# A decoder trunk on one core: how the first head's wait is filled, and who turns the second norm's first token tile

## The chip, the core and the metric

The kernel runs on one core of a Trainium2 chip. The metric is the device time of one execution in microseconds (us). TensorE is called PE here, VectorE DVE, ScalarE ACT, GpSimd POOL and SyncE SP, as in the profile.

## What is computed

With a depth of one, the trunk is one attention layer, a SwiGLU feed-forward layer and a last norm, over 512 tokens of width 2048 in float32:

```python
hn = rmsnorm(x, mix_norm_g)
h = x + nsa_mixer(hn, rel_bias, ...)      # 16 heads, 4 groups
h = h + swiglu(rmsnorm(h, ffn_norm_g), ffn_w_in, ffn_w_out)
return rmsnorm(h, final_norm_g)
```

Each head of the mixer has three branches (compressed, selected, window). Their probabilities are weighted by gates and multiplied with the values; the heads' outputs go through `w_out`. The feed-forward part needs the normed `h` with its channels on the partitions, so every token tile of 128 x 2048 must be turned once after the second norm.

## The kernel before

Every float32 product is made of three matmuls of split operands: `three` (lines 342 to 346) multiplies high by high, high by low and low by high. A weight tile (a granule of 128 x 1024) is loaded, copied to its high part on ACT (L102) and to its low part on DVE (L103) by `Weights.split`. `Weights.ahead(n)` splits until n granules beyond the one in use are ready, and issues the loads of the next three on the queue `W.queue`; `take` calls it.

The mixer's second stage interleaves two things by hand. The dense stream (`dense`) is a generator of projections for later heads: it yields after each chunk (three matmuls of 512 columns, or six of 256), counts 650 ns for it, and has 32 chunks in each pair of query heads, keys or values. `pump(h, step)` draws chunks until their count reaches a goal that grows by 20800 ns for each head of 12 steps, so one head takes exactly 32 chunks. The attention of a head is a chain:

- `scores(h, t)`: PE writes the scores of token tile t into the PSUM tile `s`, which all tiles share; DVE adds the bias and finds the maximum (L907), and ACT takes the exponential (L909).
- `finish(h, t)`: DVE scales the probabilities and turns them in blocks of 32 x 32 (L922), and SP stores them to DRAM (`d_p`, L924).
- `fetch(t)`: a DMA brings them back with the blocks in place (`ptr`, L928).
- `turn(h, b, kt)`: ACT makes the high part (`pth`, L945), DVE the low part (`ptl`, L949).
- `values(h, b, kt)`: PE multiplies with the values into `o`.

For head 0 this chain has no head before it. The kernel calls its four `scores` in a row with `pump(-1, ...)` between them, which gives 3, 3, 2 and 2 chunks, then 4 before the first scores of head 1 and 5 after them. The loop over heads draws nothing more until step 4 of head 0. `W.queue` is POOL from before the first scores on, and POOL also issues the fetches of tiles 3 and 2 of head 0.

The second norm follows the output projection. For each token tile t, four PSUM banks take the last heads' products (48 matmuls), `add` puts them on the residual `acc`, ACT sums the squares, `rstd` makes the factor and `scaled` (L314) writes the normed tile to `xn`. The next tile's matmuls are interrupted twice by `turned`, which transposes eight blocks of 128 x 128 of the tile before on PE (L322); ACT and DVE split the result into `n2_hl` (L328, L333). Tile 3 is turned inside the first feed-forward projection, which reads tiles 0 and 1 first.

Of the kernel before, what the change touches and what calls it, by code (L numbers as in the profile page):

```python
# [10 lines left out]
F32 = mybir.dt.float32  # L11
# [32 lines left out]
TP_GAP, HN_GAP = 40, 48  # L44
RESYNC = 14
PT_STEP = 224
SPREAD, N_WARM = UL, 17


# [166 lines left out]
def nsa_block(ctx: ExitStack, tc: tile.TileContext, x, rel_bias, mix_g, ffn_g, fin_g, w_in, w_out,  # L216
# [25 lines left out]
    d_o = [dram.tile([4, 128, S], F32, name=f"d_o{i}") for i in range(3)]  # L242
    d_h = dram.tile([S, 256 * N_SPILL], F32, name="d_h")
    d_r = dram.tile([NT, 128, D], F32, name="d_r")
    d_a = dram.tile([NF // 2, 128, 5 * S], F32, name="d_a")
    d_w = {j: dram.tile([128, 4, 2, 256], F32, name=f"d_w{j}") for j in G1 + G2}

# [34 lines left out]
    def tok(t):  # L282
        return slice(128 * t, 128 * (t + 1))
# [22 lines left out]
    def rstd(ss):  # L306
        y = smallp.tile([128, 1], F32, name="rs")
        run(rstd_steps(ss, y))
        return y
# [427 lines left out]
    with ExitStack() as st2:  # L737
# [22 lines left out]
        def qpair(h0):  # L760
            ps = proj2()
            end = q_out(ps, h0)
            for i in range(4):
                last = ws(ps, i, W.take(), end=end)
                for n, c in enumerate(last):
                    yield c
                    if h0 == H - 2 and i and n in (2, 4, 6):
                        reload_o(3 * i + n // 2 - 4)
                    if h0 == H - 2 and i == 3 and n in (0, 3):
                        split_o(n // 3)  # L770
            done["n"] += 1
            yield None
# [78 lines left out]

        def pump(h, step):
            at = h + (step + 4) / STEPS
            goal = 20800 * min(at, 13) + 22500 * max(at - 13, 0)
            while done["ns"] < goal:
                c = next(stream, "end")
                if c == "end":
                    return
                done["ns"] += c or 0
# [112 lines left out]
                split_from(o, hn_h[:, h], hn_l[:, h])  # L972
            del HS[h]

        W.queue = pool
        load_bias(0)
        load_bias(1)
        for i in range(4):
            scores(0, 3 - i)
            if i > 1:  # L980
                fetch(5 - i, pool)
            if i:
                finish(0, 4 - i)
            pump(-1, min(9 + i, 11.7))
        finish(0, 0)
        fetch(1)
        fetch(0)
        pump(0, 1)
        scores(1, 3)
        for b in range(2):  # L990
            turn(0, b, 3)
        pump(0, 3)
        for h in range(H):
            seq = [(b, kt) for kt in (3, 2, 1, 0) for b in (0, 1)] + [(-1, 0)]
            for i in range(STEPS):
                if i == 4:
                    load_bias(h + 2)
                if i == 2 and h:
                    fetch(0)
                if i < 9 and (h or i > 1):  # L1000
                    turn(h, *seq[i])
                if i == 8 and h + 1 < H:
                    fetch(3)
                    fetch(2)
                if i == 11 and h + 1 < H:
                    fetch(1)
                if i == 0 and h:
                    finish(h, 0)
                if h + 1 < H:
                    if i == 2:  # L1010
                        drain_to(needed(h + 1))
                    if i % 3 == 2 and h + i > 2:
                        scores(h + 1, 3 - i // 3)
                    elif i % 3 == 0 and i:
                        finish(h + 1, 4 - i // 3)
                if 2 <= i < 10 or i == 11:
                    if i == 2 and h % HPG == 0:
                        drain_to(h)
                    values(h, *seq[min(i - 2, 8)])
                    if i == 11:  # L1020
                        head_out(h)
                pump(h, i)
        W.queue = nc.sync
        drain_to(100)
    mixer.close()
# [27 lines left out]
    with tc.tile_pool(name="n2", bufs=1) as n2:  # L1053
        act(warm, epsc, AF.Sqrt)
        gb2 = n2.tile([128, D], F32, name="gb2")
        nc.scalar.dma_start(gb2, ffn_g[0:1, :].to_broadcast([128, D]))
        xn = n2.tile([128, D + 64], F32, name="xn")
        wr_h = n2.tile([128, 6, 1024], F32R, name="wr_h")
        wr_l = n2.tile([128, 6, 1024], F32R, name="wr_l")
        for i in range(6):  # L1060
            W.place[marks[0] + i] = wr_h[:, i], wr_l[:, i]
        for cb in (2, 3):
            po = out_tiles()
            cs = [slice(256 * c, 256 * (c + 1)) for c in (2 * cb - 4, 2 * cb - 3)]
            parts = [n2.tile([128, 1024], F32, name="back", bufs=3).rearrange("p (t c) -> p t c", t=NT) for _ in cs]
            for i in range(6):
                if i == 2:
                    for c, p in zip(cs, parts):
                        nc.sync.dma_start(p, d_h[:, c].rearrange("(t p) c -> p t c", p=128))
                w = W.take(2 if cb == 2 else min(2 + i, 6))  # L1070
                for t in range(NT):
                    tokmajor(po[t], w, heads(i), i == 0, i == 5, t)
            W.ahead(3)
            for t in range(NT):
                add(t, cb, po[t])
            for c, p in zip(cs, parts):
                dve.tensor_tensor(acc[:, :, c], acc[:, :, c], p, op=OP.add)
        w8 = []
        for t in range(NT):
            ss = smallp.tile([128, 4], F32, name="ss4")  # L1080
            po = out_tiles()
            for cb in range(4):
                for i in range(2):
                    if t == 0:
                        w8.append(W.take(7 - len(w8)))
                    tokmajor(po[cb], w8[2 * cb + i], heads(6 + i), i == 0, i == 1, t)
                add(t, cb, po[cb])
                if t == NT - 1 and cb == 3:
                    W.ahead(3)
                if cb == 3:  # L1090
                    pool.dma_start(d_r[t], acc[:, t])
                if t and cb in (1, 2):
                    turned(xn, (2 * cb - 2, 2 * cb - 1), t - 1)
                junk = ps3.tile([128, 512], F32, name="pp")
                act(junk, acc[:, t, 512 * cb:512 * (cb + 1)], AF.Square, accum_out=ss[:, cb:cb + 1])
            next(ready_made)
            scaled(acc[:, t], rstd(ss), gb2, xn)
            W.ahead(min(t, 2))
        firstp.close()
        pf0 = ctx.enter_context(tc.tile_pool(name="pf0", bufs=2, space=PSUM))  # L1100
        pa = [ps3.tile([128, 512], F32, name="pp") for _ in range(2)]
        gs = []
        for i in range(4):
            gs.append(W.take(min(2, 3 - i)))
            run(ws(pa, i, gs[i], 0, 256, of=n2_hl))
            if i in (1, 2):
                turned(xn, (2 * i - 2, 2 * i - 1), 3)
        act(warm, epsc, AF.Silu)
# [628 lines left out]
```

## Time and profile before

| | |
|---|---|
| median of 3 runs | 2097.61 us (2096.29 to 2098.01) |
| the profiled execution | 2096.34 us |
| its span, first to last instruction | 2094.6 us |
| around the span | 1.74 us |
| PE busy | 2075.1 us (99%) |
| DVE busy | 1627.6 us (78%) |
| ACT, POOL busy | 948.6 us (45%), 278.2 us (13%) |
| DMA, mean | 204 GB/s |

Matmuls are pipelined: the record of one lasts longer than its share of the engine. In the timeline the distance between two starts is what counts, and a stall is the part of that distance beyond the usual one. A bracket at the end of a timeline row gives the idle time before it and what ended it.

### The profile page before, as it was taken

The page shows a single profiled execution, that of the slowest core. Times are in us where ns is not written, and L with a number is a line of the kernel's source. Part 1 is how long each engine was busy: PE and PEld are TensorE (multiplying, and loading weights), DVE is VectorE, ACT ScalarE, POOL GpSimd, SP SyncE. Part 2 cuts the span into 40 slices and gives each one's busy share as a digit, 9 for nine tenths or more (in the row PEclk, how much of TensorE's full clock was granted, in tenths as well). Part 3 has the DMA queues.
Part 4 walks back from the last instruction along what each step waited for, and adds up shares of the span by engine and source line. Part 5 has one row for each costly group of instructions (what it writes and reads, how often), then busy time and mean ns, then how long its engine had stood idle before and what let it go on. Part 6 is the DMA issues. An engine that isn't in the chain of part 4 may idle for free.

```text
span 2094.6 us, 39078 instructions
## 1 busy us (share of the span) xinstructions
PE 2075.1 (99%) x15236; PEld 1954.1 (93%) x15236; DVE 1627.6 (78%) x2705; ACT 948.6 (45%) x1524; POOL 278.2 (13%) x404
## 2 busy tenths in 40 slices
PE   9999999999999999999999999999999999999998
PEld 7898788898989889899999999999999999999997
DVE  5565777777786457898888888888888688697767
ACT  6344554555455234434434344344343455464445
POOL 2000111111111001022222132221211100000000
PEclk9999999999999999999999999999999999999999
DMA  7555767666677658578878778788755686685667
GB/s 238 171 157 155 198 192 201 189 193 191 204 218 208 240 179 213 151 209 231 216 205 224 205 223 220 196 232 215 199 158 157 208 267 187 194 295 151 196 204 279
DMA packets 321799, 427.68 MB, mean 204 GB/s; under 512 B 40300, under 2 KB 249900, under 8 KB 320973
## 3 DMA queue, kind: packets, MB, share of 16 engines
q1 hardware_dynamic: 261020, 292.18, 43.9%
q0 software_dynamic: 59696, 131.16, 25.8%
q8 instruction: 119, 1.95, 0.4%
q10 hardware_dynamic: 896, 1.84, 0.2%
q14 instruction: 68, 0.55, 0.1%
HBM read 363.12 MB, written 130.13 MB: 235 GB/s over the span
## 4 chain that ended last, share of the span: by engine, by line
PE 67%; DVE 1%; DMA 1%; ACT 0%; issue 0%; SPq 0%; DVEq 0%; ACTq 0%
PE f L344 18%; PE f L345 18%; PE f L346 18%; PE proj L344 2%; PE proj L346 2%; PE proj L345 2%; PE pp L344 1%; PE pp L346 1%; PE pp L345 1%; PE po L346 1%; PE po L344 1%; PE po L345 1%; DMA tlo<-d_w 1%; PE pp L322 0%; DMA tlo<-in_ffn_w_out 0%
## 5 line engine op out<-in xcount | busy, mean ns | idle before, releaser
L103 DVE TENSOR_TENSOR wlo<-raw,whi 128x1024 fp32r<-128x1024 f32 (+2 forms) x223 | 247.5, 1112 | 123.6 <-ACT whi L102 123.0
L102 ACT ACTIVATE whi<-raw 128x1024 fp32r<-128x1024 f32 (+2 forms) x223 | 215.9, 970 | 218.8 <-PE f L346 57.0
L346 PE MATMUL f<-hn_h,wlo 128*128 128x256 f32 x984 | 271.6, 276 | 0.0
L344 PE MATMUL f<-hn_h,whi 128*128 128x256 f32 x984 | 271.6, 276 | 0.0
L345 PE MATMUL f<-hn_l,whi 128*128 128x256 f32 x984 | 271.6, 276 | 0.0
L1229 ACT ACTIVATE whi<-raw 128x1024 fp32r<-128x1024 f32 x123 | 126.2, 1058 | 303.0 <-DVE raw L1125 299.6
L1125 DVE TENSOR_TENSOR tlo<-tt,thi 128x1536 fp32r<-128x1536 f32 (+1 forms) x83 | 145.4, 1752 | 77.8 <-ACT thi L1234 77.3
L344 PE MATMUL proj<-hn_h,whi 128*128 128x512 f32 x504 | 199.9, 397 | 0.0
L346 PE MATMUL proj<-hn_h,wlo 128*128 128x512 f32 x504 | 196.9, 391 | 0.0
L345 PE MATMUL proj<-hn_l,whi 128*128 128x512 f32 x504 | 196.9, 391 | 0.0
L345 PEld LDWEIGHTS f<-hn_l,whi 128*128 128x128 f32 x984 | 184.7, 188 | 0.0
L344 PEld LDWEIGHTS f<-hn_h,whi 128*128 128x128 f32 x984 | 184.7, 188 | 0.0
L346 PEld LDWEIGHTS f<-hn_h,wlo 128*128 128x128 f32 x984 | 184.7, 188 | 0.0
L1234 ACT ACTIVATE thi<-tt 128x1536 fp32r<-128x1536 f32 x82 | 121.9, 1486 | 72.9 <-PE f L345 61.3
L345 PE MATMUL f<-tlo,slot 128*128 128x256 f32 (+1 forms) x546 | 151.7, 278 | 0.0
L344 PE MATMUL f<-thi,slot 128*128 128x256 f32 (+1 forms) x546 | 151.6, 278 | 0.0
L346 PE MATMUL f<-thi,slot 128*128 128x256 f32 (+1 forms) x546 | 151.6, 278 | 0.0
L346 PE MATMUL proj<-whi,hn_l 128*128 128x256 f32 (+2 forms) x496 | 146.1, 295 | 2.9 <-DVE hn_l L810 2.9
L1125 DVE TENSOR_TENSOR wlo<-raw,whi 128x1024 fp32r<-128x1024 f32 x123 | 147.0, 1223 | 1.1 <-ACT whi L1229 1.1
L344 PE MATMUL proj<-whi,hn_h 128*128 128x256 f32 (+2 forms) x496 | 146.6, 295 | 0.8 <-ACT hn_h L809 0.8
L345 PE MATMUL proj<-wlo,hn_h 128*128 128x256 f32 (+2 forms) x496 | 145.6, 294 | 0.0
L345 PE MATMUL f<-wlo,slot 128*128 128x256 f32 (+1 forms) x432 | 121.4, 281 | 0.0
(406 smaller groups left out, 6459.9 us busy)
## 6 DMA issues: line engine op xcount, KB each, us to landing
raw<-in_ffn_w_in SPq DMA_DIRECT2D x135, 512.0 KB, 5.1
d_w<-in_ffn_w_out POOLq DMA_DIRECT2D x80, 512.0 KB, 8.4
rawx<-in_ffn_w_in SPq DMA_DIRECT2D x41, 512.0 KB, 4.8
raw<-in_ffn_w_out SPq DMA_DIRECT2D x73, 256.0 KB, 3.9
tlo<-d_w SPq DMA_DIRECT2D x73, 256.0 KB, 4.3
d_a<-d_a POOLq DMA_DIRECT2D x120, 128.0 KB, 5.7
slot<-d_a SPq DMA_DIRECT2D x18, 768.0 KB, 6.7
raw<-in_nsa_w_in POOLq DMA_DIRECT2D x24, 512.0 KB, 5.0
```

Source lines behind the costliest of these rows:

```text
L102: self.nc.scalar.activation(hi[:, :n], src, AF.Copy)
L103: self.nc.vector.tensor_tensor(lo[:, :n], src, hi[:, :n].bitcast(F32), op=OP.subtract)
L344: mm(o, ah, bh, start=start, stop=False, skip_group_check=True)
L345: mm(o, ah, bl, start=False, stop=False, skip_group_check=True)
L346: mm(o, al, bh, start=False, stop=stop, skip_group_check=True)
L1125: dve.tensor_tensor(o, a, b, op=OP.subtract)
L1229: act(h, r, AF.Copy)
L1234: act(h, ttf, AF.Copy)
```

## The change

Two edits. The first head's filling: the chunks between the four scores become 4, 2, 3 and 2, then 4, then 7 after the first scores of head 1, and `pump` draws again from step 2 of head 0 on. A lead of 3900 ns, which shrinks to nothing at head 13, is added to the goal of `pump`. The raw weights of this stretch are loaded on SP; POOL takes over after it. One granule's split is moved by hand from a `take` to a call of `W.ahead(2)` after the last scores of head 0.

The second norm's first tile: `first_turned` writes the normed tile in an order of channels such that DVE's transposition of 32 x 32 blocks (128 x 2048 in one instruction), four stores to DRAM and one load put the channels on the partitions. The load goes to `acc[:, 0]`, which is free after its own store to `d_r`. `first_hi` then makes both parts, two instructions on ACT and two on DVE, at the end of tile 2 and inside tile 3. The 16 transposes of this tile on PE and its splits go away. Two calls of `W.ahead` are shifted to make room.

```diff
+LEAD = 3900
+    d_n = dram.tile([4, 32, 4, 512], F32, name="d_n")
-                last = ws(ps, i, W.take(), end=end)
+                last = ws(ps, i, W.take(1 if h0 == 2 and i == 1 else 2), end=end)
         def pump(h, step):
             at = h + (step + 4) / STEPS
-            goal = 20800 * min(at, 13) + 22500 * max(at - 13, 0)
+            pump_to(20800 * min(at, 13) + 22500 * max(at - 13, 0) + LEAD * max(1 - at / 13, 0))
-        W.queue = pool
         load_bias(0)
         load_bias(1)
         for i in range(4):
             scores(0, 3 - i)
             if i > 1:
                 fetch(5 - i, pool)
             if i:
                 finish(0, 4 - i)
-            pump(-1, min(9 + i, 11.7))
+            if i == 3:
+                W.ahead(2)
+            pump_to(650 * (4, 6, 9, 11)[i])
         finish(0, 0)
         fetch(1)
         fetch(0)
-        pump(0, 1)
+        pump_to(650 * 15)
         scores(1, 3)
         for b in range(2):
             turn(0, b, 3)
-        pump(0, 3)
+        pump_to(650 * 22)
+        W.queue = pool
...
-                pump(h, i)
+                if h or i > 1:
+                    pump(h, i)
...
+        def first_turned(y):
+            v = xn[:, :D].rearrange("p (m k j) -> p k m j", m=4, j=32)
+            a, g = (x.rearrange("p (k m j) -> p k m j", m=4, j=32) for x in (acc[:, 0], gb2))
+            for m in range(4):
+                dve.scalar_tensor_tensor(v[:, :, m], a[:, :, m], y, g[:, :, m], op0=OP.mult, op1=OP.mult)
+            b = back[:, :2].rearrange("p b c -> p (b c)")
+            dve.transpose(b, xn[:, :D])
+            for a in range(4):
+                nc.sync.dma_start(d_n[:, :, a].rearrange("m j f -> j m f"),
+                                  b[32 * a:32 * a + 32].rearrange("j (m f) -> j m f", m=4))
+            nc.sync.dma_start(acc[:, 0], d_n.rearrange("m j a f -> (m j) (a f)"))
+        def first_hi():
+            v = acc[:, 0].rearrange("p (a k s) -> p k a s", a=4, s=32)
+            h, l = (x[:, :, tok(0)].rearrange("p k (a s) -> p k a s", a=4) for x in n2_hl)
+            k2 = (slice(0, 8), slice(8, 16))
+            for k in k2:
+                act(h[:, k], v[:, k], AF.Copy)
+            for k in k2:
+                dve.tensor_tensor(l[:, k], v[:, k], h[:, k].bitcast(F32), op=OP.subtract)
+                yield
...
-                if t and cb in (1, 2):
+                if t > 1 and cb in (1, 2):
                     turned(xn, (2 * cb - 2, 2 * cb - 1), t - 1)
...
+                if t == NT - 1 and cb == 2:
+                    next(parts_of_first)
+                    W.ahead(2)
             next(ready_made)
-            scaled(acc[:, t], rstd(ss), gb2, xn)
-            W.ahead(min(t, 2))
+            if t:
+                scaled(acc[:, t], rstd(ss), gb2, xn)
+            else:
+                first_turned(rstd(ss))
+            if t == 2:
+                parts_of_first = first_hi()
+                next(parts_of_first)
+            W.ahead(min(t, 1))
```

## Rows read from the trace of the kernel before

**Rows 1.** The page, busy time of each engine with its share of the span.
```profile
PE 2075.1 (99%) x15236; PEld 1954.1 (93%) x15236; DVE 1627.6 (78%) x2705; ACT 948.6 (45%) x1524; POOL 278.2 (13%) x404
```

**Rows 2.** Waits of PE in the whole run: total us, times, longest us.
```profile
PE proj L346 <- DVE hn_l L810: 2.9, 2, 2.2
PE o L344 <- ACT pth L945: 1.7, 1, 1.7
```

**Rows 3.** Windows: stretch, length, busy us by engine, PEclk, DMA share, GB/s.
```profile
350.00:400.00 50.00, 50.00 (x245) 42.19 (x244) 39.12 (x108) 25.06 (x68) 5.99 (x8) 1.00 0.66 189
...
608.00:611.50 3.50, 3.50 (x17) 3.50 (x18) 2.16 (x8) 2.42 (x8) 0.00 (x0) 0.52 0.93 286
```

**Rows 4.** Timeline of PE, first head: start, duration, line, output<-inputs, idle before.
```profile
203.15 0.39 PE L346 MATMUL proj<-hn_h,wlo 128*128 128x512 f32 x1
204.41 0.40 PE L344 MATMUL s<-k0h,qh 128*128 128x288 f32 x1 [0.88 <-DVE mx L907]
...
209.57 0.40 PE L346 MATMUL proj<-hn_h,wlo 128*128 128x512 f32 x1
210.73 0.40 PE L344 MATMUL s<-k0h,qh 128*128 128x288 f32 x1 [0.77 <-DVE mx L907]
...
216.77 0.39 PE L344 MATMUL proj<-hn_h,whi 128*128 128x512 f32 x1
...
219.97 0.39 PE L346 MATMUL proj<-hn_h,wlo 128*128 128x512 f32 x1
220.98 0.30 PE L344 MATMUL o<-pth,v0h 128*128 128x128 f32 x1 [0.62 <-issue]
...
221.76 0.28 PE L346 MATMUL o<-pth,v0l 128*128 128x128 f32 x1
223.70 0.38 PE L344 MATMUL o<-pth,v0h 128*128 128x256 f32 x1 [1.66 <-ACT pth L945]
224.16 0.39 PE L345 MATMUL o<-ptl,v0h 128*128 128x256 f32 x1
```

**Rows 5.** Timeline of DVE, first head.
```profile
210.59 0.08 DVE L907 DVE_READ_ACCUMULATOR2_ANT mx<- 128x1 f32 x1
...
220.91 0.49 DVE L949 TENSOR_TENSOR ptl<-ptr,pth 128x128 fp32r<-128x128 f32 x2 [1.22 <-ACT pth L945]
```

**Rows 6.** Timeline of ACT (first row) and POOL, first head.
```profile
223.23 0.72 ACT L945 ACTIVATE pth<-ptr 128x256 fp32r<-128x256 f32 x2 [1.20 <-DMA ptr<-d_p]
...
217.56 0.76 POOL L928 DMA_DIRECT2D ptr<-d_p  x1 [2.35 <-DMA d_p<-p]
218.31 1.52 POOL L86 DMA_DIRECT2D raw<-in_nsa_w_in  x2
```

**Rows 7.** Timeline of PE, second norm, tile 1 and the first feed-forward projection.
```profile
773.46 0.39 PE L346 MATMUL proj<-wr_h,hn_l 128*128 128x512 f32 x1
773.69 1.03 PE L322 MATMUL pp<-ident,xn 128*128 128x128 f32 x8
774.48 0.48 PE L344 MATMUL po<-wr_h,hn_h 128*128 128x512 f32 x1
...
812.36 0.81 PE L322 MATMUL pp<-ident,xn 128*128 128x128 f32 x6
```

**Rows 8.** DVE: transposition durations min/median/max ns; then the second norm's timeline.
```profile
L922 DVE STREAM_TRANSPOSE p<-p x64: 578/980/1381, 208.5 to 676.5; 128x1152 f32<-128x1152 f32 x16, 128x896 f32<-128x896 f32 x16, 128x640 f32<-128x640 f32 x16, 128x384 f32<-128x384 f32 x16
...
771.38 2.74 DVE L314 SCALAR_TENSOR_TENSOR xn<-acc,rs,gb 128x512 f32<-128x512 f32 x4
...
806.90 0.69 DVE L1039 TENSOR_TENSOR acc<-acc,po 128x512 f32<-128x512 f32 x1 [1.13 <-PE po L346]
...
810.09 2.74 DVE L314 SCALAR_TENSOR_TENSOR xn<-acc,rs,gb 128x512 f32<-128x512 f32 x4
```

**Rows 9.** DMA issues: output<-input, queue, count, KB each, us to landing (203 to 230, 765 to 800).
```profile
d_p<-p SPq DMA_DIRECT2D x4, 48.0 KB, 5.5
...
d_r<-acc POOLq DMA_DIRECT2D x3, 1024.0 KB, 5.2
```

More of the change, by code (lines that the diff above doesn't have):

```diff
@@ L853, in pump, with pump_to @@
             at = h + (step + 4) / STEPS
-            goal = 20800 * min(at, 13) + 22500 * max(at - 13, 0)
+            pump_to(20800 * min(at, 13) + 22500 * max(at - 13, 0) + LEAD * max(1 - at / 13, 0))
+        def pump_to(goal):
             while done["ns"] < goal:
@@ L1057, in nsa_block @@
         xn = n2.tile([128, D + 64], F32, name="xn")
+        back = n2.tile([128, 3, 1024], F32, name="back")
+        n_back = iter((0, 1, 2, 0))
+        def first_turned(y):
[18 more added lines that the diff above has]
+                yield
         wr_h = n2.tile([128, 6, 1024], F32R, name="wr_h")
@@ L1064, in nsa_block @@
             cs = [slice(256 * c, 256 * (c + 1)) for c in (2 * cb - 4, 2 * cb - 3)]
-            parts = [n2.tile([128, 1024], F32, name="back", bufs=3).rearrange("p (t c) -> p t c", t=NT) for _ in cs]
+            parts = [back[:, next(n_back)].rearrange("p (t c) -> p t c", t=NT) for _ in cs]
             for i in range(6):
```

## The prediction

> **What bounds the kernel.** I read the page first: PE is busy for 2075.1 of 2094.6 us [rows 1], so 19.5 us of idle time is all that a better order can give back, and anything beyond it must take work off PE. Then the waits of PE, which put names to the idle time [rows 2], and the timeline of PE around the two edits, where starts are compared, because a matmul of 512 columns follows the one before by 0.23 us (773.46 to 773.69 [rows 7]) although its record is 0.39 long. A chunk of the dense stream is three such matmuls, 0.69 us. Last, the timelines of the engines that released PE [rows 5, 6, 8].
>
> In the first head PE stalls four times [rows 4]. Before the scores of tile 2: 204.41 − 203.15 − 0.23 = 1.03. Before those of tile 0: 210.73 − 209.57 − 0.23 = 0.93. Before the first values: 220.98 − 219.97 − 0.23 = 0.78. Before the third values: 223.70 − 221.76, less the 0.11 that a matmul of 128 columns takes, is 1.83, and the next matmul starts another 0.46 later where 0.12 would do, 0.34 more. In all 4.9 us. The first two end when DVE has read the last maximum out of the shared PSUM tile, the last two when `pth` and `ptl` are there. In the second norm PE doesn't stall; it spends 774.48 − 773.69 = 0.79 us on each group of eight transposes [rows 7].
>
> **Part 1, the first head's filling.** Three of the four stalls are answered by more chunks in front of them; none of the chain of attention is shortened. So I keep the times of DVE, ACT and the DMAs and move only PE.
>
> The stall before tile 2 shrinks by one chunk, 1.03 − 0.69 = 0.34, but tile 1 now has two chunks ahead of it, not three, and what PE wins comes back as waiting until 210.59, when DVE leaves the maximum of tile 1 [rows 5]. DVE's order is the same up to there (the split that was drawn by the ninth chunk would now fall ahead of a `finish`; the diff moves it by hand to where it was). So PE stands at 210.73 as before, with nine chunks done and not eight: gain 0.69.
>
> From there 2 and 4 chunks follow, as before, and PE is through with head 1's first scores at 216.77. Seven chunks, not five, last until 216.77 + 7 × 0.69 = 221.6. The first `ptl` pair begins at 220.91 and lasts 0.49 [rows 5], so it is ready at 221.4: the stall of 0.78 goes. Two groups of values (6 × 0.11) and the three new chunks of step 3 bring PE to 221.6 + 0.7 + 2.1 = 224.4. The `pth` pair that ended the longest stall starts at 223.23 and ends at 223.95 [rows 6]; PE started on its first half at 223.70 before. So 1.83 + 0.34 go too, with 0.7 us to spare for the first half. Part 1 gives 0.69 + 0.78 + 2.17 = 3.6 us. If the third values are late by all that they were, 1.5; if the first two stalls go as well, 4.9.
>
> The moves between queues cost nothing in this sum. POOL loses two loads, which were issued at 218.31, behind the fetch at 217.56 [rows 6]. On SP the first of them stands behind the stores of tile 1 and ahead of those of tile 0, which wait for DVE's next transposition anyhow; the second stands behind the last fetch and is wanted only three granules (24 chunks, over 16 us) later. Issued sooner, the first takes part of the transfer time of that fetch. The row shows 223.23 − 217.56 = 5.7 us from issue to ACT's start, with a weight load alongside already. It may lose nothing, or up to the 0.7 us of slack and then as much of the 2.17 as it is late.
>
> By the Trainium skill ("Trainium Kernel Development and Optimization", Key Constraints) DMAs issued on the queues of SP, ACT and POOL share the same 16 engines, so another queue saves issue time alone. By that rule the load competes with the fetch on either queue, and the second rival below gets its chance from it.
>
> **The lead.** It doesn't add work: six chunks are drawn sooner and fewer per head later, 300 ns of 20800. Before, 20800 / 650 = 32 chunks make one head and one unit, so each split and each end of a unit falls on the same step in every head; afterwards it is 31.5, and they wander over the steps until head 12. The stretch 350 to 400 shows PE busy for 50.00 of 50 us with DVE at 39.12 [rows 3], so DVE has 22% to absorb a burst. I take nothing. A gain is excluded while PE is full; a loss is bounded by a stall as in rows 2 (1.7 at most for a late `pth`) in each head. From step 6 of head 12 on, by the formula of the goal, the chunks are where they were; just before that, one split comes a step sooner.
>
> **Part 2, the first tile of the second norm.** PE loses two groups, 2 × 0.79 = 1.6 us, in line with the matmuls and on the path. What replaces them is beside it. DVE: the four scalings stay (2.74 from 771.38 [rows 8]); the transposition of 2048 columns isn't in the trace, the same instruction takes 1381 ns for 1152 columns and 578 for 384, so 1.05 ns a column and about 2.3 us for 2048. It delays the sums of tile 1, whose banks are wanted a whole tile later ((810.09 − 771.38) / 3 = 12.9 us by the scalings of tiles 0 and 3 [rows 8]): hidden. The tile is turned by 771.4 + 2.7 + 2.3 = 776.4. Four stores: up to 5.5 us, as small ones took among weight loads; the load of 1 MB: 5.2, as `d_r` of that size took the other way [rows 9]. It lands near 787. It is wanted at the end of tile 2, one tile before the last scalings: 810.1 − 12.9 − 1.6 = 795.6. Eight us to spare.
>
> Last, DVE in tile 3: the second half of `first_hi` and one split now stand ahead of the last sum, each like a split of 1.2 us, and only 1.13 us of idle time is there [rows 8], so the scaling of tile 3 comes some 1.3 later against PE. It began at 810.09; PE's transposes of that tile began at 812.36 [rows 7], and two of four scalings (1.37) must be through for all eight: 0.9 to spare. It may lose 0.4; the first four need one scaling only, so I take nothing. Part 2 gives 1.6, at worst 1.2.
>
> **Sum.** 3.6 + 1.6 = 5.2. The profiled execution takes 2096.34, of which 1.74 lie around the span, so it becomes 2091.1 (span 2089.4). It is 1.27 below the median; from the median I get 2097.61 − 5.2 = 2092.4. Its own range, from the bounds of both parts and 0.5 of the runs' spread, is 2090.5 to 2094.0. A measurement of this kernel can tell about 0.2%, 4.2 us, from no change: faster means below 2093.4, slower above 2101.8.
>
> **Rivals.**
> 1. The fetch stays late. The third values wait as long as before, because the load moved to SP takes what the chunks give: 2092.4 + 2.2 = 2094.6. For it: PE's wait ended with a DMA [rows 6]. Against: 0.7 of slack, and only half of a 512 KB load moves by some 1 us. 15%.
> 2. The wandering splits make new stalls, and the kernel gets slower. Place: heads 1 to 12, where a split on ACT and DVE falls between the exponentials and `pth`. Price: the longest wait for `pth`, 1.7 [rows 2]. It ends slower from (4.2 + 5.2) / 1.7 = 6 heads on; in all twelve it is 2092.4 + 20.4 = 2112.8; in two or three it only eats the gain, 2096 to 2097.5. For it: DVE is at 78% there. Against: values are drawn two steps (about 5 us) after their `pth`. 15%, of which 5% slower.
> 3. A late stretch gets better by accident. At 608 to 611.5 the granted clock is 0.52, near the lower of its two levels, 1.2 GHz, with PE busy throughout [rows 3]; before it PE waited 2.2 us for `hn_l` (2.9 in two waits [rows 2]). The split that moves by a step lies just ahead. At half the clock 3.5 us hold 1.7 too many. Without both: 2092.4 − 1.7 − 2.2 = 2088.5. The same neighbourhood may also get worse by some us, which the range holds. 12%.
> 4. The turned tile comes too late, and ACT, with the squares of tile 3 queued behind, makes PE wait. With a load of three times 5.2 it lands 2 us late: 2094.4. The Trainium skill ("VectorE: DVE Perf Modes", The three transpose paths) warns that a DMA copy which transposes by strides is 19 times slower than the DMA's own transposition where the innermost stride is large, and its Rules for kernel authors give whole 128 x 128 blocks to TensorE. By that factor on the row's 5.2 the load takes 99 us, PE waits over 75 and the kernel ends near 2170. But DVE turns the elements and the DMAs move runs of 512 floats, and the fetch of rows 6 is of that kind with 5.7 us. 3%, 1% for the extreme.
> That the change doesn't do what it says isn't left open: 16 fewer instructions on PE and the count of chunks are in the code.
>
> **How the numbers follow.** The forecast has 55%: 46% below 2093.4, 9% above. Faster: 46 + 12 = 58%. Same: 9 + 15 + 10 + 2 = 36%. Slower: 5 + 1 = 6%. The range reaches from rival 3 (2088.5) to two or three new stalls (2097.5).
>
> **What would show it.** Right: 48 `pp` transposes, not 64; the stalls before the first and third values gone; the two at 204.4 and 210.7 still there, smaller; PE full from 225 to 590. Wrong: a `pth` ended by a DMA in front of PE (rival 1), brackets on `o` or `s` rows in heads 1 to 12 (2), another picture at 595 to 612 (3), ACT idle for `acc` in tile 2 (4).

## The result and the profile after

| | before | after |
|---|---|---|
| median | 2096.43 us (2095.66 to 2098.01, 5 runs) | 2115.49 us (2113.64 to 2118.05, 5 runs) |
| span of the profiled execution | 2094.6 us | 2113.8 us |

The changed kernel is slower: ratio 1.0089, 95% interval 1.0074 to 1.0104. The forecast was 2092.4, a little faster.

The page's busy times of the kernel after, to be read against [rows 1]:

```profile
PE 2082.0 (98%) x15220; PEld 1955.8 (93%) x15220; DVE 1630.7 (77%) x2704; ACT 948.9 (45%) x1522; POOL 275.6 (13%) x400
```

Its waits of PE (total us, times, longest us), against [rows 2]:

```profile
PE o L347 <- DVE ptl L953: 8.8, 12, 1.7
PE o L346 <- ACT pth L949: 7.6, 7, 2.1
PE proj L348 <- DVE hn_l L812: 2.1, 4, 0.8
```

Before, the row of `ptl` was:

```profile
PE o L345 <- DVE ptl L949: 1.5, 3, 0.8
```

PE has 16 instructions fewer, as the code says. Its idle time is 31.8 us where it was 19.5, and it is busy for 6.9 us more with less work. The values `o` wait for `pth` and `ptl`, 16.4 us where it was 3.2, and that is the whole growth of the idle time. Some 5 us of the growth of the busy time are clock: behind such waits it is near half of full speed in three stretches that the kernel before doesn't have (0.55 from 242.0 to 245.4, 0.52 from 488.0 to 491.5, 0.57 from 522 to 526), and each holds 1.5 to 1.7 us too many. The rest of it wasn't taken apart.

Next, where along the run the time is lost. The last values matmul of each head (`o<-pth,vcc` in the timeline of PE) is a mark that all kernels share. The distance to the kernel before at a mark holds the chunks that are drawn ahead, 0.69 us each and counted from the trace; without them it is what is lost. (It is good to about half a us: the same code starts the row `s` of tile 2 in [rows 4] at 203.87 in one execution and 204.68 in another.)

| mark | before, at | after | chunks ahead | lost |
|---|---|---|---|---|
| end of head 0 | 242.53 | +4.65 | 5 | 1.2 |
| head 1 | 272.23 | +5.71 | 5 | 2.3 |
| head 7 | 451.41 | +7.88 | 2 | 6.5 |
| head 9 | 511.35 | +16.10 | 1 | 15.4 |
| head 12 | 603.65 | +22.16 | 0 | 22.2 |
| head 13 | 640.96 | +20.48 | 0 | 20.5 |
| output projection | 757.36 | +20.60 | 0 | 20.6 |
| feed-forward | 806.70 | +18.85 | 0 | 18.9 |

The second norm wins 1.75 us, from +20.60 to +18.85. The loss lies in the heads. Timeline of PE of the kernel after, first head, against [rows 4]:

```profile
204.24 0.39 PE L348 MATMUL proj<-hn_h,wlo 128*128 128x512 f32 x1
204.81 0.40 PE L346 MATMUL s<-k0h,qh 128*128 128x288 f32 x1 [0.19 <-DVE mx L911]
...
210.23 0.39 PE L348 MATMUL proj<-hn_h,wlo 128*128 128x512 f32 x1
211.12 0.40 PE L346 MATMUL s<-k0h,qh 128*128 128x288 f32 x1 [0.50 <-DVE mx L911]
...
221.70 0.39 PE L348 MATMUL proj<-hn_h,wlo 128*128 128x512 f32 x1
221.93 0.22 PE L346 MATMUL o<-pth,v0h 128*128 128x128 f32 x1
...
224.44 0.39 PE L348 MATMUL proj<-hn_h,wlo 128*128 128x512 f32 x1
224.67 0.28 PE L346 MATMUL o<-pth,v0h 128*128 128x256 f32 x1
...
235.14 0.39 PE L346 MATMUL o<-pth,v0h 128*128 128x512 f32 x1
236.21 0.50 PE L347 MATMUL o<-ptl,v0h 128*128 128x512 f32 x1 [0.69 <-DVE ptl L953]
...
238.59 0.39 PE L348 MATMUL proj<-hn_h,wlo 128*128 128x512 f32 x1
240.37 0.49 PE L346 MATMUL o<-pth,v0h 128*128 128x512 f32 x1 [1.39 <-ACT pth L949]
241.18 0.50 PE L347 MATMUL o<-ptl,v0h 128*128 128x512 f32 x1 [0.31 <-DVE ptl L953]
```

Up to 225 all goes as forecast: the stalls before the scores are smaller, the first and the third values start 0.23 after the matmul before them. Then, at the values of the key tile that is multiplied last and is the widest (512 columns), there are stalls that the kernel before didn't have: 0.84, 1.55 and 0.58 us. By the end of head 0 what was won is gone, and 1.2 us more; the low clock from 242.0 on has 1.5 in it.

The same picture comes back later, larger. Timeline of ACT of the kernel after, head 8:

```profile
477.91 0.19 ACT L913 ACTIVATION_READ_ACCUMULATOR p<-u,mx 128x1 f32 x1
478.01 1.04 ACT L103 ACTIVATE whi<-raw 128x1024 fp32r<-128x1024 f32 x1
478.95 0.62 ACT L949 ACTIVATE pth<-ptr 128x512 fp32r<-128x512 f32 x1
483.92 0.63 ACT L371 ACTIVATE qh<-yt 128x512 fp32r<-128x512 f32 x1 [4.35 <-DVE yt L398]
484.46 1.04 ACT L103 ACTIVATE whi<-raw 128x1024 fp32r<-128x1024 f32 x1
485.41 0.61 ACT L949 ACTIVATE pth<-ptr 128x512 fp32r<-128x512 f32 x1
```

Of DVE in the same time:

```profile
479.08 1.23 DVE L104 TENSOR_TENSOR wlo<-raw,whi 128x1024 fp32r<-128x1024 f32 x1 [1.85 <-ACT whi L103]
480.22 0.68 DVE L953 TENSOR_TENSOR ptl<-ptr,pth 128x512 fp32r<-128x512 f32 x1
...
482.20 1.11 DVE L926 STREAM_TRANSPOSE p<-p 128x896 f32<-128x896 f32 x1
483.24 0.65 DVE L398 SCALAR_TENSOR_TENSOR yt<-proj,ybc 128x512 f32<-128x512 f32 x1
```

And of PE:

```profile
483.56 0.39 PE L348 MATMUL proj<-hn_h,wlo 128*128 128x512 f32 x1
486.07 0.51 PE L346 MATMUL o<-pth,v0h 128*128 128x512 f32 x1 [2.13 <-ACT pth L949]
```

A unit is here what 32 chunks make, a pair of query heads, keys or values; it has two halves, each of which is scaled when its sum is complete. Read the rows from the end. PE waits for the second `pth` (485.41). On ACT this stands behind `qh`, the scaled queries that close one half of a unit, and a `whi` of the chunk after it; `qh` waited 4.35 us for DVE's `yt`. On DVE, `yt` stands behind `finish` (the transposition at 482.20), and that behind a granule's `wlo`, for which DVE idled 1.85 us, because its `whi` on ACT stood behind the exponentials of the scores.

The same place of head 8 in the kernel before, ACT:

```profile
470.34 0.62 ACT L945 ACTIVATE pth<-ptr 128x512 fp32r<-128x512 f32 x1
470.87 1.04 ACT L102 ACTIVATE whi<-raw 128x1024 fp32r<-128x1024 f32 x1
471.81 0.61 ACT L945 ACTIVATE pth<-ptr 128x512 fp32r<-128x512 f32 x1
476.44 0.63 ACT L369 ACTIVATE qh<-yt 128x512 fp32r<-128x512 f32 x1 [4.01 <-DVE yt L396]
```

and DVE:

```profile
472.98 1.11 DVE L922 STREAM_TRANSPOSE p<-p 128x896 f32<-128x896 f32 x1
474.01 1.18 DVE L103 TENSOR_TENSOR wlo<-raw,whi 128x1024 fp32r<-128x1024 f32 x1
```

There ACT waits for `yt` as long, but both `pth` are through before it, and `wlo` comes behind `finish` and waits for nothing. So none of these instructions takes more than 0.05 us longer than before; it is their order in the two queues. Two kinds of the stream's work now lie ahead of what PE wants next: the **end of a unit's half** (`yt`, `qh`, `ql`, drawn with chunks 28 and 32 of a unit's 32) and a granule's **split** (`whi`, `wlo`, drawn with chunks 9, 17, 25 and 29).

### The profile page after: what moved, and what is told of

It reads as the page before. It is cut to its first block, busy times and chain, and to the rows that moved or that the text cites. A ratio compares the mean times of both kernels' runs of the same rounds, so it can differ in the third digit from the quotient of the medians.

```text
span 2113.8 us, 39065 instructions
## 1 busy us (share of the span) xinstructions
PE 2082.0 (98%) x15220; PEld 1955.8 (93%) x15220; DVE 1630.7 (77%) x2704; ACT 948.9 (45%) x1522; POOL 275.6 (13%) x400
## 4 chain that ended last, share of the span: by engine, by line
PE 67%; DVE 1%; ACT 0%; DMA 0%; issue 0%; DVEq 0%; ACTq 0%
PE f L347 19%; PE f L346 19%; PE f L348 19%; PE proj L346 2%; PE proj L348 2%; PE proj L347 2%; PE pp L348 1%; PE pp L347 1%; PE pp L346 1%; PE po L346 1%; PE po L348 1%; PE po L347 1%; DMA tlo<-in_ffn_w_out 0%; PE pp L324 0%; DVE slot L1171 0%; PE o L347 0%
```

## The experiments

Each was measured beside the kernel before, whose median in these batches was 2097.1 to 2098.3 us. Every diff is against the kernel before or after, as named.

**Which edit.** e1 is the kernel before with the second norm's hunks alone; e2 has those of the first head alone; e3 is e2 without the lead:

```diff
-LEAD = 3900
+LEAD = 0
```

> The kernel before with the second norm's edit alone. All theories of the first edit say the same here, since nothing of it is in: 16 transposes fewer on TensorE, 1.6 to 1.8 us off, about 2094.7 against 2096.4, with the stage before the second norm unchanged and the first feed-forward projection 1.75 us sooner, as between the two traces. If the second edit has a cost that the first one hid, the time is above the kernel before.

> The first head's filling, the lead and the queue alone; the second norm as before. If the two edits are independent, it is 1.75 us above the changed kernel: about 2117, ratio 1.0095 to 1.010, with the loss in heads 0 to 13. If the loss needs both edits (more traffic on SP's queue), it is below 2105.

> The first head's filling and the queue, with the lead set to nothing, so that from step 5 of head 0 on each step draws the chunks that it drew before. Theory of the order (the lead moves the end of each unit of the dense stream ahead of a turn, whose high part then waits on ScalarE behind the unit's): heads 1 to 13 show no stalls that were not there before, and 2 to 3 us of the first head's 4.9 are won, about 2094. Theory of the queue (weights on SP delay stores and fetches): the loss stays, near 2115.

Measured: e1 2096.86 us, ratio 0.9997 (0.9988 to 1.0005); e2 2117.56, 1.0090 (1.0076 to 1.0104); e3 2095.97, 0.9990 (0.9982 to 0.9999). The whole loss is in the first head's edit, and in it in the lead. In e3 the heads 1 to 13 have no new stall, so neither the queue nor the other goals cost. Its first head is 2.09 us sooner, with 0.86 and 0.56 left at the third values. e1's gain from the output projection to the feed-forward is 1.67 us by the marks. Its time alone doesn't show a gain (the interval goes from 2.5 us faster to 1.0 slower), and its profiled execution had lost 2.4 in the first head, told of below.

**Is it the lead, or the steps that it changes?** The kernel before, one chunk more or fewer ahead in heads 1 to 11, still 32 chunks per head:

```diff
+            goal += 650 if 1 <= at < 12 else 0      # e4
+            goal -= 650 if 1 <= at < 12 else 0      # e5
```

> The kernel before with one chunk of lead, 650 ns, from step 8 of head 0 to step 8 of head 11, and nothing else. 32 chunks still make a head. Theory of the order: the 28th chunk of each unit, which ends its first half, falls into step 6 and so ahead of the turn of step 7, in every one of eleven heads; a stall of 1 to 3 us in most of them at the values of tile 0: 2105 to 2125. Theory of less cover (300 ns fewer per head): the number of chunks per head is as before, so no stall, 2096. Theory of the queue: 2096.

> The kernel before with one chunk fewer drawn ahead in heads 1 to 11 (the other sign of the run with one chunk more). Theory of the unit's end: chunk 28, which ends the first half of a unit and puts the scalings of the new queries or keys on DVE and ACT, then falls as the second chunk of step 7 and so still behind the `turn` of that step; no `pth` comes late, no stall at the first values of a step, and the time is that of the kernel before, 2095 to 2099, ratio 0.999 to 1.001. Theory that each step away from the old meeting of the two streams costs, in either direction: stalls of 1 to 1.7 in heads 1 to 11 again, 2110 or more, ratio 1.006 or more.

Measured: e4 2122.76 us, 1.0113 (1.0097 to 1.0128), slower than the change itself; e5 2103.85, 1.0030 (1.0018 to 1.0043). One chunk, 0.69 us of work done sooner and given back, costs 25 us, so it isn't less cover and isn't the wandering as such. In e5, where I expected nothing, PE stalls for 0.5 to 0.8 in nine heads at values of 128 columns (`ptl`, 10 waits, 5.0 us of idle time in all): the unit's second half there closes a step later, and its `yt` and `k1l` stand in front of a tile's maxima on DVE.

**Two suspects, one at a time and together.** The kernel before with one chunk moved from step 7 to 6 (e9: the end of the first half falls ahead of the `turn` of step 7), from step 6 to 5 (e10: a split falls ahead of `finish`), or both (e11):

```diff
+            goal += 650 if step == 6 and 1 <= h < 12 else 0         # e9
+            goal += 650 if step == 5 and 1 <= h < 12 else 0         # e10
+            goal += 650 if step in (5, 6) and 1 <= h < 12 else 0    # e11
```

> The kernel before, with one chunk moved from step 7 to step 6 in heads 1 to 11 and all other chunks where they were. That chunk is the one that ends the first half of a unit; the granule's split that lies ahead of it stays on its side of `finish`. Theory of the unit's end (ACT stands at the scaling of the queries with the `pth` of step 7 queued behind it): this alone brings stalls at the first values of step 7 in most of the eleven heads, 1 to 1.7 each, so 10 us or more, 2107 to 2120. Theory of the split (a split that falls ahead of `finish` delays everything behind it on DVE): under 5 us, below 2102.

> The kernel before, with one chunk moved from step 6 to step 5 in heads 1 to 11, so that the split of a granule that is drawn with it falls ahead of the `turn` and the `finish` of step 6, while the end of the unit stays in step 7, behind the `turn`. Theory of the unit's end: no more than 5 us, below 2102, and no late `pth` at step 7. Theory of the split: 10 us or more, 2107 or more.

> The kernel before with both of the two moves that were made singly: in heads 1 to 11 one chunk goes from step 6 to step 5 (its split then lies ahead of `finish`) and one from step 7 to step 6 (the end of the unit then lies ahead of the `turn` of step 7). Theory that the two costs add: 3.1 + 4.8 = 7.9 us, 2105 to 2107. Theory that they meet (the split makes DVE wait for ACT ahead of `finish`, the queries' scaling then comes after both, and the `pth` of step 7 waits on ACT for all three): the full price of the run with one chunk more, stalls of 1 to 1.7 and 0.58 at the first two values of 512 in most heads, 18 to 25 us, 2115 to 2123.

Measured: e9 2100.93 us, 1.0017 (1.0008 to 1.0026); e10 2102.69, 1.0025 (1.0014 to 1.0036); e11 2106.34, 1.0041 (1.0028 to 1.0053). Neither theory got its price: 3, 5 and 9 us, about the sum, and far from 25. In e9 the end does what was feared, but `pth` is just in time. ACT of e9, head 6:

```profile
418.66 0.63 ACT L369 ACTIVATE qh<-yt 128x512 fp32r<-128x512 f32 x1 [3.92 <-DVE yt L396]
419.19 0.62 ACT L946 ACTIVATE pth<-ptr 128x512 fp32r<-128x512 f32 x1
```

and PE, which waits for `ptl` alone:

```profile
419.93 0.43 PE L344 MATMUL o<-pth,v1h 128*128 128x512 f32 x1
420.67 0.50 PE L345 MATMUL o<-ptl,v1h 128*128 128x512 f32 x1 [0.30 <-DVE ptl L950]
```

What e4 has beyond e11 are a head's other splits, a chunk sooner. Before, chunks 9, 17 and 25 are the first of steps 0, 3 and 6, and their splits lie behind the `finish` of these steps; one chunk sooner (or two) all three are drawn in steps 11, 2 and 5, which have `scores`, behind the exponentials. A view shows it: DVE's wait for `whi` in the stretch 240 to 590, in the kernel before (total us, times, longest us):

```profile
DVE wlo L103 <- ACT whi L102: 3.5, 11, 0.5
```

in the kernel after:

```profile
DVE wlo L104 <- ACT whi L103: 30.8, 23, 2.3
```

in e4:

```profile
DVE wlo L103 <- ACT whi L102: 69.0, 44, 2.3
```

and in e13, the next kernel:

```profile
DVE wlo L104 <- ACT whi L103: 3.4, 11, 0.5
```

e4's 33 waits beyond those of before are three in each of eleven heads, of (69.0 − 3.5) / 33 = 2.0 us. In the kernel after, 5.0 of the 30.8 us come before 450 and 25.8 after it, when the lead is down to two chunks and one.

**A lead of eight.** Eight chunks use up one granule, so the splits of chunks 9, 17 and 25 move to steps 9, 0 and 3, again the first behind a `finish`, while both ends come eight chunks sooner, and the split of chunk 29 with them. The kernel after, the lead kept to head 12 (e13) or to the end (e14):

```diff
-LEAD = 3900
+LEAD = 5200
-... + LEAD * max(1 - at / 13, 0))
+... + LEAD * min(max(13.5 - at, 0) / 1.5, 1))      # e13
+... + LEAD)                                        # e14
```

> The changed kernel with a lead of eight chunks (5200 ns) that stays as it is from the first head to the middle of head 12 and is given back until the middle of head 13. Eight chunks are one granule, so each split falls on the step where it fell before, and the end of a unit falls on step 4, where it stands to the `finish` of step 3 and the `turn` of step 4 as it stood to those of steps 6 and 7. Theory of the order: from head 1 to head 11 the distance to the kernel before stays within 1 us, however large the lead; the first head's gain may then be kept, 2091 to 2094. Theory that a lead costs by itself (less cover in each head, or units and loads that come too soon): the distance grows by 10 us or more from head 1 to 11, 2105 or more.

> The same with the lead of eight chunks kept to the end of the stream, so that the chunks run out eight sooner in the last heads. Heads 1 to 11 as with the lead that is given back. If the last heads have cover to spare, 2090 to 2094; if not, the eight chunks come back there as idle time of PE, up to 8 x 0.69 = 5.5 us, 2094 to 2099.

Measured: e13 2113.36 us, 1.0075 (1.0063 to 1.0088); e14 2117.19, 1.0092 (1.0079 to 1.0106). My expectation had gone by the first end only. With the splits in place (3.4 us in the row above) the distance still grows by 19 us from head 1 to head 11 (+3.28 to +22.47). Timeline of ACT of e13, head 1:

```profile
265.46 0.61 ACT L371 ACTIVATE k1h<-yt 128x512 fp32r<-128x512 f32 x1
265.98 0.62 ACT L949 ACTIVATE pth<-ptr 128x512 fp32r<-128x512 f32 x1
```

and of PE:

```profile
270.43 0.50 PE L347 MATMUL o<-ptl,v0h 128*128 128x512 f32 x1 [0.64 <-DVE ptl L953]
```

The second end (265.46) now lies ahead of both wide `pth` of the head, where before it came behind them.

**Ends put back.** A list holds the closing instructions of a half (queries, keys or values) until step 7 for the first half and step 8 for the second; chunks and splits are drawn where they were. On the kernel after (e15), on e13 (e16), on e4 (e17):

```diff
-                    end(u)
+                    later(u, end, u)
...
+    def later(u, f, *a):
+        if clock[0] is not None and 3 <= clock[0] < 7 + u:
+            held.append((u, f, a))
+        else:
+            f(*a)
...
+                at_step(i)      # ahead of pump(h, i), issues what is due
```

> The changed kernel with its lead; all chunks and splits are drawn where they were, but the instructions that end a half of a unit (the scalings of new queries, keys and values on DVE and ACT) are held back where they come early: those of the first half until step 7, behind its `turn`, those of the second until step 8. Theory of the ends: the stalls at the values of 512 go down to what the split alone cost, 0.5 at most per head, and the time is 2092 to 2099. Theory of the splits: those wander as before, the stalls stay, 2108 or more. Theory of the lead itself: the same, 2108 or more.

> The lead of eight chunks that is given back in heads 12 and 13, with the ends of the units held until steps 7 and 8. Splits and ends both fall where they fell before the change. Theory of the ends: no stalls in heads 1 to 11, the distance to the kernel before stays within 1 us there, and the end is at 2091 to 2095. Theory of the lead itself (less cover, other loads): 10 us and more come in heads 1 to 11 as without the holding, 2105 or more.

> The kernel before with one chunk more ahead in heads 1 to 11 and the ends of the units held until steps 7 and 8; the splits come a chunk sooner, and stay so. Without the holding this cost 25 us. Theory of the ends: what is left is the split's share, some 5 us as where a split alone was moved, 2099 to 2104. Theory of the splits: 2112 or more. If ends and splits cost only where they meet, as little as 2097 to 2100.

Measured: e15 2105.94 us, 1.0037 (1.0025 to 1.0050); e16 2095.15, 0.9986 (0.9977 to 0.9995); e17 2120.79, 1.0109 (1.0094 to 1.0125). These tell the causes apart. The splits are called in phase where they fall on the steps on which the kernel before has them. With the splits in phase, holding the ends takes 18 us off e13: from head 1 to head 10 it goes from +1.40 to +0.73 with eight chunks ahead throughout. With the splits out of phase by one, holding them takes 2 us off e4, and 22 us are left, without a stretch of low clock in heads 1 to 11. This is put down to the splits, which come a step sooner three times a head; no run moves them back with the chunks left where they are. One such split by itself cost 5 us (e10). Why three cost more than thrice that wasn't taken apart. e17's row of DVE shows how one of them idles (`wlo` ahead of `ptl` and `finish`), as head 8 did:

```profile
392.30 1.23 DVE L103 TENSOR_TENSOR wlo<-raw,whi 128x1024 fp32r<-128x1024 f32 x1 [1.84 <-ACT whi L102]
```

e15 divides the changed kernel. At the end of head 0 it is at −0.28 with five chunks ahead, so 5 × 0.69 + 0.28 = 3.7 us are won there, where the kernel after lost 1.2. In heads 1 to 7 (+0.76 with two chunks ahead at the end) it loses 3.1, and in heads 8 to 12 (+10.19 with none) another 10.8: there the splits are one or two chunks sooner than before. (The profiled execution of e16 took 4004.48 us, because its granted clock is 0.16 from 1700 us on; only its marks up to 700 us are read, and the 2095.15 is the median of all its runs.)

**A fixed lead, given back later.** The lead of six kept to head 12 (e19) or 13 (e20), and the lead of eight kept to head 13 (e18), all with the ends held; the formula of the goal is e13's with 13.5 for e19 and 14.5 for the others, and `LEAD` stays 3900 for the six.

> The changed kernel with the ends held back and the lead kept at six chunks from head 0 to the middle of head 12, then given back until the middle of head 13. Six chunks ahead, each split is the third chunk of a step with `finish` and stays behind it; one or two ahead, it would be drawn in a step with `scores`, behind its exponentials. Theory of the meeting (only the offsets of one and two cost): heads 1 to 11 stay within 1 us of head 0's distance, where the falling lead lost 8 us in heads 7 to 11, and the end is at 2092 to 2096. Theory that splits out of phase cost at any offset: as with one chunk more and the ends held, 1.5 us a head and more, 2108 or more.

> The same with the lead given back a head later, from the middle of the stretch of heads 13 to 14.5, where PE was full and DVE busy for 14 of 20 us. If the 3 to 4 us that are lost in giving back belong to the tight stretch of head 12, they are kept: 2091 to 2094. If they belong to the giving back (fewer chunks in a head whose chain of attention sets its length), they go there as well, or more: 2094 to 2098.

> The lead of eight with the ends held, given back in heads 13 to 14.5 as well. Place: 2090 to 2093. Giving back: eight chunks are missed more than six, 2095 to 2100.

Measured: e19 2098.50 us, 1.0005 (0.9996 to 1.0014); e20 2097.44, 1.0001 (0.9992 to 1.0010); e18 2090.94, 0.9968 (0.9955 to 0.9980). e19 goes from +0.23 to +2.92 in the ten heads with six chunks ahead, less than e17's 22 and more than nothing, so an offset of six costs little though not none; DVE waits for `whi` there for 20 us in the same stretch, which shows that the wait alone isn't the price. That it costs where something due stands behind it is argued from the rows above. But giving the lead back in head 12 brings none of its 6 × 0.69 = 4.1 us (+2.74 at the end of head 13), and in head 13 only some (e20, +2.79 after head 10, +1.11 after head 14). With eight, given back in heads 13 to 14.5 (e18), the distance goes from +1.62 at the end of head 12 to −4.29 at that of head 15. Why eight do better there than six wasn't taken apart.

e18 is faster than both kernels. The view of waits has no row of PE for it from 240 to 590. The part that isn't full is head 12. Window of e18 (stretch, length, busy us by engine, granted clock, DMA share, GB/s):

```profile
590.00:620.00 30.00, 24.75 (x179) 23.24 (x178) 24.90 (x62) 16.78 (x40) 3.00 (x4) 0.94 0.70 216
```

**Both edits with little or no lead.** The kernel after with goals of its own in head 0 only (e8), and with a lead of nothing (e12):

```diff
-LEAD = 3900
+EARLY = {3: 24, 4: 25, 5: 26}    # e8: chunks drawn by these steps of head 0, no lead after
+LEAD = 0                         # e12
```

> The changed kernel with both edits, but the lead only inside head 0: the goals of its steps 3, 4 and 5 are 24, 25 and 26 chunks, and from step 6 on the goal is that of the kernel before, so that head 1 starts with no chunk drawn ahead. If the lead that lasts through twelve heads is the whole cost, the heads 1 to 12 show no new stalls, the first head keeps most of its 3 to 4 us, the second norm its 1.75: 2092 to 2094, ratio 0.998 to 0.9985. If the chunks won in the first head can't be kept without the lead, 2094 to 2096. If the wandering wasn't the cause, 2110 or more.

> The changed kernel with a lead of nothing: both edits otherwise as they are. If the two parts add, the 1.3 to 1.9 us of the first head's edit without the lead and the 1.75 of the second norm come together: 2097.6 less 3.0 to 3.7, 2093.9 to 2094.6, ratio 0.998 to 0.9987, and no new stalls in heads 1 to 12.

Measured: e8 2095.19 us, 0.9989 (0.9980 to 0.9998); e12 2095.66, 0.9992 (0.9983 to 1.0001). The wandering gone, the loss of 19 us is gone. Less of the first head's gain is kept: without a lead the chunks won there are missed later in the same head. e8 trades the stall at the third values for 0.64 and 0.44 us at 235 and 240. In e12's profiled execution the third values wait 2.22 us: no chunk is drawn just in front of them, and the fetch takes 6.31 us to the row of `pth`, the longest of all runs.

## Why the prediction was wrong

The step that failed is **"The lead … I take nothing"**. Its facts were right: fewer chunks per head, splits and ends of units on other steps. Its reason was wrong. It argued from averages, PE full and DVE at 78% of a stretch [rows 3], that a burst would be absorbed. But in these rows each queue is worked off in order, `pth` behind a `qh` for which ACT idled 4.35 us, and the kernel before had three of a head's four splits right behind a `finish`, and both ends behind a wide `turn` that they would have delayed; DVE's rows there hold 3.5 us of waiting for `whi` in 350 us. The mean load said nothing of that. The bound beside it, one stall of 1.7 at most in each head, was wrong as well: head 8 alone loses 4.8 us, head 9 4.2 and head 12 4.3, by several stalls and the low clock behind them. To see it one had to follow a single head on ACT and DVE and ask, for each split and end, what stands behind it if it comes a step sooner.

**Rival 2** had the right place, and its own sign, brackets on `o` rows in heads 1 to 12, is what the trace shows. That its 2112.8 for twelve stalls of 1.7 lies near the measured 2115.5 is luck: heads 3 to 5 lose nothing, head 8 nearly three such stalls, and head 0's gain is gone as well, which it left in. It had 15%, a third of that for slower. It named the splits only. Measured, they cost most of what heads 8 to 12 lose (10.8 of 15.7 us, by e15), and the ends the larger part of the rest: 2115.49 − 2105.94 = 9.6 us between the kernel after and e15. Some 5 of these 9.6 are low clock: e15's profiled execution has none of the three stretches at 242, 488 and 522. The argument against it, that values are drawn two steps after their `pth`, was no protection: the slack was there, 5 us long, and ACT alone waited 4.35 of them for `yt`.

**Part 1** was right in mechanism and near in size up to 225 us. PE reaches the third values at 224.67, where 224.4 was forecast. The third values' stall is gone with its `pth` where it was (ACT):

```profile
223.36 0.72 ACT L949 ACTIVATE pth<-ptr 128x256 fp32r<-128x256 f32 x2 [0.93 <-DMA ptr<-d_p]
```

That is 0.13 later than in [rows 6], so rival 1 (the one that the prediction's paragraph on the queues calls the second) fell. The move to SP isn't free: from the fetch's issue on POOL to this row it is 4.95 to 6.31 us, median 5.6, in the twelve kernels that load on SP, and 4.77 to 5.67, median 5.05, in the eight that load on POOL. The half us is covered by the 0.7 of slack in the forecast. The Trainium skill ("Trainium Kernel Development and Optimization", Key Constraints) lets the queues share the DMA engines; these times agree in that the fetch got no faster when the loads went to another queue. What I had left out is that chunks drawn ahead are only won if a later step doesn't miss them. Forecast 3.6 us; won in head 0 with the ends held, 3.7 (e15) and 8 × 0.69 − 1.47 = 4.05 (e18), and 4.3 at the end of the heads in e18; in the changed kernel nothing is left, since the stalls at 235 to 241 and the low clock behind them gave it all back.

**Part 2** was right: 1.75 us by the marks, forecast 1.6. DVE of the kernel after (scalings and transposition of the first tile), against [rows 8]:

```profile
791.97 2.74 DVE L1073 SCALAR_TENSOR_TENSOR xn<-acc,rs,gb 128x512 f32<-128x512 f32 x4
794.75 2.31 DVE L1075 STREAM_TRANSPOSE back<-xn 128x2048 f32<-128x2048 f32 x1
```

ACT, taking up the turned tile:

```profile
814.96 2.01 ACT L1087 ACTIVATE hn_h<-acc 128x1024 fp32r<-128x1024 f32 x2
```

PE, a group of transposes that is left, against [rows 7]:

```profile
805.17 1.03 PE L324 MATMUL pp<-ident,xn 128*128 128x128 f32 x8
805.96 0.48 PE L346 MATMUL po<-wr_h,hn_h 128*128 128x512 f32 x1
```

and the stores to DRAM (KB each, us to landing), against [rows 9]:

```profile
d_n<-back SPq DMA_DIRECT2D x4, 256.0 KB, 3.9
```

The transposition takes 2.31 us (2.3 forecast), the stores 3.9, and ACT takes the turned tile up with no wait for a DMA, so rival 4 fell as well. A group of eight transposes still costs PE 0.79. The Trainium skill ("VectorE: DVE Perf Modes", The three transpose paths and Rules for kernel authors) would leave 128 x 128 blocks to TensorE and warns of strided DMA copies; here DVE's 32 x 32 blocks and DMAs of whole runs did it beside a full PE, and the measurement decides for this place.

**Rival 3** occurred only in part: the longest wait for `hn_l` is 0.8 us, no longer 2.2, but there are four (2.1 us in all), the granted clock is still 0.59 from 620.5 to 624.5, and a wait of 1.70 for `ptl` at 617 is new. Nothing is won there; e18 keeps the idle time as well (24.75 of 30 us busy).

The range has a slip of its own: its upper end, 2094.0, doesn't follow from the bounds of the parts, since 1.5 + 1.2 us off 2097.61 is 2094.9, and 2095.4 with the half us of spread. It changes nothing here. The sum itself, 3.6 + 1.6 = 5.2 us, is near what e18 brings at the feed-forward, 5.97, where little stands in the way.

## What to carry to other kernels

Where two streams of work share engines that run in order, look at what the filler stream puts in the queue at each step, before shifting it: one chunk of 0.69 us cost 25 us here. Shift by a whole period of the filler's side work (eight chunks here), and pin its closing work to the step where it was harmless (the shift alone 2113.4 us, e13; with the pinning 2095.2, e16, and given back a head later 2090.9, e18). A mean load below 80% is no proof of slack; follow one iteration of the loop, row by row, on the engines that feed the bottleneck.

## What the runs showed of the hardware

The granted clock of PE can fall to near the lower of its two levels, 1.2 GHz, after a cluster of stalls, with PE busy throughout the stretch at the low clock. Windows of the kernel after:

```profile
488.00:491.50 3.50, 3.50 (x10) 2.71 (x9) 2.26 (x8) 2.32 (x7) 0.00 (x0) 0.52 0.48 153
...
242.00:245.40 3.40, 3.40 (x10) 2.67 (x9) 2.48 (x12) 2.39 (x7) 0.00 (x0) 0.55 0.58 183
```

Ahead of these PE had waited 2.13 and 0.84 us, and 0.69, 1.39 and 0.31. At 0.52 of full speed 3.5 us hold some 1.7 us too many, more than half of what the two waits ahead of them took. It doesn't always fall: head 7 of the kernel after has waits of 0.90 and 0.84 us at 453.6 and 454.9, and the granted clock stays at 1.00 from 454 to 464. Nor is it settled by the stalls alone: e1 has the same first three stalls as the kernel before (1.03, 0.92 and 0.78, where before has 1.03, 0.93 and 0.78), and in this stretch of e1's profiled execution the granted clock is 0.50

```profile
223.00:226.50 3.50, 3.19 (x8) 2.47 (x9) 3.38 (x9) 1.12 (x3) 1.50 (x2) 0.50 0.77 219
```

and 1.00 in that of the kernel before. That is where e1's profile lost its 2.4 us. What decides it, no run here shows.
